# Six of the 2-MB weight loads of a mixture-of-experts kernel go out in three parts

## The chip, the cores and the metric

The kernel runs on one core of a Trainium2 chip. The metric is the device time of one execution in microseconds (us); lower is better. Three timed runs of the kernel before took 1313.0 to 1313.3 us, with a median of 1313.22 us. KB and MB in the rows are those of the profile: a load of "2048.0 KB" is 2,097,152 bytes.

## What is computed

One layer of a decoder over 512 tokens of width 1024: an attention part with two branches, then a mixture of 64 experts of which each token uses two, then a last norm. Cut to what the change is about:

```
def expert_block(args):            # D = 1024, D_EXPERT = 512
    xb, e = args
    return (jax.nn.silu(xb @ w1[e]) * (xb @ w3[e])) @ w2[e]

def reference(x, ...):
    h = rms_norm(x, attn_norm);  x = x + hybrid_mixer(h, ...)   # w_in, w_proj_fox, w_proj_swa, w_out
    h = rms_norm(x, ffn_norm);   x = x + hier_moe(h, ...)       # group top-1, expert top-2, expert_block
    return rms_norm(x, final_norm)
```

w1 and w3 are (64, 1024, 512), w2 is (64, 512, 1024), all float32: 2 MB for each matrix of each expert, 192 such matrices, 403 MB in all. Every one of them is read once.

## The kernel before

The first third of the span is the attention part. The experts follow in 16 batches of four (b = 0 to 15). Each expert has 32 token slots, so four experts fill the 128 partitions. A batch takes twelve 2-MB matrices: w1 of four experts (e = 0 to 3), w3 of four, w2 of four. TensorE multiplies them in float32 (`h` at L1571 from w1 and w3, `y_ps` at L1608 from w2), with the weights as the moving operand, and adds the batch's results to the token rows (`c_ps`, L1368).

The weights come from HBM by DMAs that SyncE (SP) issues in program order. `load_next` (L1028) issues one matrix as one DMA at L1038: 128 partitions, each a contiguous piece of 16 KB in HBM (for w1, partition p holds rows 8p to 8p+7). So a load is 128 packets of 16 KB. The tile comes from one of three rings (2, 4 and 2 tiles, `RING`), eight 2-MB tiles in all; a DMA into a tile waits until TensorE has read what was there before. `load_ahead` at the start of a batch issues as many loads as the rings allow. Batch 0 and the last batch's w2 are loaded in smaller parts by other functions. The landing of DMAs is told by eight semaphores in turn (DMAHW0 to DMAHW7 in the listings below): each DMA takes the next one and first waits for the DMA that had it before, eight DMAs earlier.

Other transfers that the prediction reads from: `raw_pf` (512 KB, 128 partitions) and `raw_ps` (twice 256 KB, 64 partitions each), both loaded at L174 in pieces of 1 KB as parts of the projection weights, and `fkl<-c_k` (L739), which moves four partitions of 2 KB within the core.

Of the kernel before, what the change touches and what calls it, by code (L numbers as in the profile page):

```python
# [20 lines left out]
P = 128  # L21
# [23 lines left out]
ANGLES_AT = 6  # L45
FORGET_AT = 13
ROUNDS = (5, 3)

CUTS = ((0, 512), (512, 768), (768, 1024))
BIG = 3e38  # L50
# [46 lines left out]
def kernel(ctx: ExitStack, tc: tile.TileContext, a: dict, out: bass.AP, dbg=None):  # L97
    nc = tc.nc
# [849 lines left out]
    w1, w3, w2 = a["w1"][0], a["w3"][0], a["w2"][0]  # L948
# [16 lines left out]
    def weights(m, x, k):  # L965

        w, n = {"w1": (w1, NC), "w3": (w3, NC), "w2": (w2, 4)}[m]
        rows = w[x].rearrange("(p c) n -> p c n", c=n)
        return rows if k is None else rows[:, k * n // 2:(k + 1) * n // 2]

    def note(b, m, k, e, rows):

        if k is None:
            wt[b, m, e] = rows
        else:
            wt.setdefault((b, m, e), [None] * (2 * len(rows)))[k * len(rows):(k + 1) * len(rows)] = rows

    def load_half(t, b, m, k, e):

        if (b, m, k) == (N_BATCH - 1, "w2", 1):  # L980

            src = w2[4 * b:4 * b + 4].rearrange("x (p c) n -> p c x n", c=4)
            if e < 2:
                t = t.rearrange("p (x n) -> p x n", x=4)
                nc.sync.dma_start(t, src[:, 2 + e, :, slice(*CUTS[0])])
                last[0, 2 + e] = [t[:, x] for x in range(4)]
                return
            t = t.rearrange("p (u x n) -> p u x n", u=2, x=4)
            for u in range(2):
                nc.sync.dma_start(t[:, u], src[:, 2 + u, :, slice(*CUTS[e - 1])])  # L990
                last[e - 1, 2 + u] = [t[:, u, x] for x in range(4)]
            return
        t = t.rearrange("p (c n) -> p c n", c=2 if m == "w2" else 4)
        nc.sync.dma_start(t, weights(m, 4 * b + e, k))
        note(b, m, k, e, [t[:, c] for c in range(t.shape[1])])
# [34 lines left out]
    def load_next():  # L1030

        i = len(issued) - n_first
        issued.append(i)
        t = rings[next_places[i % n_ring]].tile([P, 4096], F32, tag="ring", name=f"load{i}")
        if len(loads[i]) == 1 and loads[i][0][2] is None:
            b, m, k, e = loads[i][0]
            t = t.rearrange("p (c n) -> p c n", c=4 if m == "w2" else NC)
            nc.sync.dma_start(t, weights(m, 4 * b + e, k))  # L1038
            note(b, m, k, e, [t[:, c] for c in range(t.shape[1])])
            return  # L1040
        for u, x in enumerate(loads[i]):
            load_half(t[:, 2048 * u:2048 * u + 2048], *x)
# [23 lines left out]
    for n in range(4):  # L1066
# [5 lines left out]
        for m, src_hi, src_lo in (("pf", lambda k: ofT[k][0], lambda k: ofT[k][1]),  # L1072
                                  ("ps", lambda k: osT_hi[:, k], lambda k: osT_lo[:, k])):
            hi, lo = halves_of[f"{m}{n}"]
            for j in range(2):
                b = 2 * n + j
# [31 lines left out]
    def x1_part(n, t, o):  # L1108

        x1 = x1s[t % 2]  # L1110
        v.tensor_tensor(x1, o, xb_of[n][:, t], op=OP.add)
        act.activation(junk, x1, AF.Square, accum_out=sq4[:, t, n:n + 1])
# [64 lines left out]
    def route_places(t):  # L1177
        for x in range(2):
            v.scalar_tensor_tensor(junk[:, 0:N_EXP], pos_ps[t], 1.0, oh[:, x, t], op0=OP.mult, op1=OP.mult,
                                   accum_out=slots[:, x, t:t + 1])  # L1180
            yield
        yield from pick(t, slots, codes)
# [97 lines left out]
    def weave(rounds=1000):  # L1280

        for _ in range(rounds):
            for g in list(live):
                if next(g, "end") == "end":
                    live.remove(g)

    def later(n, g):
        for _ in range(n):
            yield
        yield from g  # L1290

    for t in range(NT):
        o = acc_tile(f"out_ps3_{t}")[:, :256]
        for cc in range(NC):
# [8 lines left out]
            if cc == 3 and t:  # L1303
                part_logits(3, t - 1)
                live.append(route_experts(t - 1))
                if t > 1:
                    route_count(t - 2)
                    live.append(later(1, route_places(t - 2)))
                weave(ROUNDS[t == 3])
        x1_part(3, t, o)  # L1310
# [242 lines left out]
    def load_ahead(n):  # L1553
        while len(issued) - n_first < min(n, len(loads)):
            load_next()
# [101 lines left out]
```

## Time and profile before

| what | us |
|---|---|
| median of three runs | 1313.22 |
| the profiled execution, its own time | 1313.3 |
| its span, first to last instruction | 1311.3 |
| around the span | 2.0 |

| engine | busy us | share of the span |
|---|---|---|
| TensorE matmuls | 1126.6 | 86% |
| VectorE | 457.5 | 35% |
| ScalarE | 245.7 | 19% |
| GpSimd | 73.6 | 6% |

The page also has a line for the core's 16 DMA engines: the span in 40 slices, with a digit for the busy share in tenths, and under it the GB/s that were moved. A busy share near 1.00 means that all 16 engines were moving a packet nearly all of the time.

### The profile page before, as it was taken

How to read it: one execution, taken by the hardware profiler on the slowest of the kernel's cores; microseconds unless marked ns; L12 is line 12 of the kernel's file. 1: busy time of each engine (PE TensorE's matmuls, PEld its weight loads, DVE VectorE, ACT ScalarE, POOL GpSimd, SP SyncE). 2: the span in 40 equal slices, each digit the busy share in tenths (PEclk: the TensorE clock that was granted, in tenths of full speed). 3: DMA queues.
4: the chain of work that ended last, by engine and by line, in shares of the span. 5: the costliest groups of instructions: out<-in, count | busy, mean ns of one | idle time of the engine just before them, and what ended most of it. 6: DMA issues, size and time to landing. Idle time of an engine off the chain costs nothing.

```text
span 1311.3 us, 16877 instructions
## 1 busy us (share of the span) xinstructions
PE 1126.6 (86%) x6934; PEld 610.5 (47%) x6934; DVE 457.5 (35%) x1138; ACT 245.7 (19%) x559; POOL 73.6 (6%) x100
## 2 busy tenths in 40 slices
PE   8999999999999797978879696968878786967865
PEld 8987777878984262413233241413232331413212
DVE  7776666236263362212303121212313121211113
ACT  5665444433541000000000000000000000000003
POOL 2700000012000000000000000000000000000002
PEclk9999999999999899979989898989889998989878
DMA  5222231356989999999999999999999999999995
GB/s 185 76 66 74 78 88 55 96 146 202 347 280 417 427 427 426 428 427 428 427 426 428 427 427 426 428 426 428 428 426 427 421 428 424 428 426 427 428 421 190
DMA packets 70074, 438.92 MB, mean 335 GB/s; under 512 B 9878, under 2 KB 39594, under 8 KB 45036
## 3 DMA queue, kind: packets, MB, share of 16 engines
q1 hardware_dynamic: 69994, 437.82, 82.3%
q8 instruction: 56, 0.92, 0.3%
q14 instruction: 22, 0.18, 0.0%
q10 hardware_dynamic: 2, 0.00, 0.0%
HBM read 433.48 MB, written 2.10 MB: 332 GB/s over the span
## 4 chain that ended last, share of the span: by engine, by line
PE 63%; DMA 31%; DVE 3%; SPq 1%; issue 1%; ACT 1%; POOL 1%; DVEq 0%; POOLq 0%; ACTq 0%
DMA load<-in_w_dram 30%; PE h L1571 11%; PE y_ps L1608 9%; PE g_ps L1261 9%; PE c_ps L1368 8%; PE acc_g L322 2%; PE acc_g L323 2%; PE acc_g L324 2%; SPq L1038 1%; PE of_ps L823 1%; PE acc_wo L324 1%; PE acc_kv L433 1%; PE acc_wo L322 1%; PE acc_wo L323 1%; PE fpT_ps L805 1%
## 5 line engine op out<-in xcount | busy, mean ns | idle before, releaser
L1571 PE MATMUL h<-load,u_hi 128*32 128x512 f32 x1920 | 293.3, 671 | 88.3 <-DMA load<-in_w_dram 88.1
L1608 PE MATMUL y_ps<-load,u_hi 128*32 128x512 f32 x920 | 167.9, 680 | 53.6 <-DMA load<-in_w_dram 50.3
L1571 PEld LDWEIGHTS h<-load,u_hi 128*32 128x32 f32 x1920 | 69.6, 121 | 288.4 <-issue 155.9
L1261 PEld LDWEIGHTS g_ps<-u_hi,xc 128*128 128x128 f32 x1024 | 118.8, 194 | 24.6 <-issue 13.0
L1261 PE MATMUL g_ps<-u_hi,xc 128*128 128x128 f32 x1024 | 124.9, 281 | 0.6 <-DVE over L1492 0.6
L1374 DVE TENSOR_TENSOR u_lo<-c_ps,u_lo 128x512 f32<-128x512 f32 x84 | 58.1, 692 | 188.3 <-PE c_ps L1368 188.3
L1608 PEld LDWEIGHTS y_ps<-load,u_hi 128*32 128x32 f32 x920 | 40.5, 117 | 168.8 <-issue 89.3
L1267 DVE TENSOR_TENSOR u_hi<-g_ps,cst 128x512 f32<-128x512 f32 (+1 forms) x33 | 21.9, 667 | 278.1 <-PE h L1571 261.5
L1368 PE MATMUL c_ps<-xb,xb 128*128 128x512 f32 x240 | 116.7, 617 | 1.0 <-DVE u_lo L1371 0.8
L1355 ACT ACTIVATE xb<-h 128x512 f32<-128x512 f32 x16 | 9.6, 597 | 355.9 <-PE h L1571 355.9
L1368 PEld LDWEIGHTS c_ps<-xb,xb 128*128 128x128 f32 x240 | 37.8, 188 | 79.4 <-DVE u_lo L1374 36.8
L1343 POOL TENSOR_TENSOR xb<-xb,u_hi 128x512 f32<-128x512 f32 x16 | 20.4, 1273 | 824.8 <-DVE xb L1342 748.4
L1365 ACT ACTIVATE xb<-y_ps 128x512 f32<-128x512 f32 x30 | 17.9, 597 | 216.4 <-PE y_ps L1608 216.4
L1362 ACT ACTIVATE u_hi<-t_ps 128x512 f32<-128x512 f32 x16 | 9.6, 597 | 255.3 <-PE t_ps L1361 255.3
L322 PE MATMUL acc_g<-hT_hi,hi_g 128*128 128x512 f32 x128 | 54.2, 423 | 0.0
L1211 DVE TENSOR_SCALAR u_hi<-codes,locs,cst 128x128 f32<-128x128 f32 x60 | 21.8, 363 | 87.5 <-PE g_ps L1261 87.5
L323 PE MATMUL acc_g<-hT_lo,hi_g 128*128 128x512 f32 x128 | 50.5, 395 | 0.0
L324 PE MATMUL acc_g<-hT_hi,lo_g 128*128 128x512 f32 x128 | 50.4, 394 | 0.0
L1356 DVE TENSOR_TENSOR u_hi<-h,xb 128x512 f32<-128x512 f32 x16 | 16.5, 1033 | 90.0 <-PE h L1571 89.1
L189 DVE TENSOR_TENSOR lo_g<-raw_g,hi_g 128x1024 fp32r<-128x1024 f32 x16 | 19.6, 1226 | 36.1 <-ACT hi_g L187 36.1
L322 PE MATMUL acc_wo<-hi_wo,mT 128*128 128x256 f32 x96 | 28.7, 299 | 0.0
L324 PE MATMUL acc_wo<-hi_wo,mT 128*128 128x256 f32 x96 | 27.1, 283 | 0.1
(377 smaller groups left out, 1604.3 us busy)
## 6 DMA issues: line engine op xcount, KB each, us to landing
load<-in_w_dram SPq DMA_DIRECT2D x176, 2048.0 KB
first<-in_w_dram SPq DMA_DIRECT2D x16, 1024.0 KB
load<-in_w_dram SPq DMA_DIRECT2D x9, 1024.0 KB
raw_g<-in_w_in_dram SPq DMA_DIRECT2D x16, 512.0 KB
raw_wo<-in_w_out_dram SPq DMA_DIRECT2D x8, 512.0 KB
x_sb<-in_x_dram SPq DMA_DIRECT2D x4, 512.0 KB
raw_qs<-in_w_in_dram SPq DMA_DIRECT2D x4, 512.0 KB
raw_vf<-in_w_in_dram SPq DMA_DIRECT2D x4, 512.0 KB
```

The source lines that it names most:

```text
L189: defer(wait, lambda: v.tensor_tensor(lo, r, hi.bitcast(F32), op=OP.subtract))
L322: pe.matmul(o, l_hi, r_hi, start=first, stop=False, skip_group_check=True)
L323: pe.matmul(o, l_hi, r_lo, start=False, stop=False, skip_group_check=True)
L324: pe.matmul(o, l_lo, r_hi, start=False, stop=last, skip_group_check=True)
L1211: v.tensor_scalar(sel1[:, t], labels, loc[:, 0, t:t + 1], r, op0=OP.is_equal, op1=OP.mult)
L1261: pe.matmul(g_ps[k][:, c * P:(c + 1) * P], xc[t][:, 4 * k + c], sel1[:, t], start=(t, c) == (0, 0), stop=t == NT - 1, skip_group_check=True)
L1267: v.tensor_tensor(hsel[:, d], g_ps[k][:, c * P:(c + step) * P].rearrange("p (c n) -> p c n", c=step), g_ffn[:, d, None].to_broadcast([P, s ...
L1343: gp.tensor_tensor(wsel, wsel, wtmp, op=OP.add)
L1368: pe.matmul(c_ps, w_t[:, t], ys[k], start=True, stop=True)
L1374: v.tensor_tensor(d, c_ps, d, op=OP.add)
L1571: pe.matmul(o[s], hsel[:, c, s], wt[b, m, e][c], start=c == 0, stop=c == NC - 1, skip_group_check=True)
L1608: pe.matmul(y_ps[k][s], gT[:, c, s], wt[b, "w2", e][c][:, 512 * k:512 * k + 512], start=c == 0, stop=c == 3, skip_group_check=True)
```

## The change

A list names six of the loads: the w1 matrix of the third expert (e = 2) in batches 1, 4, 6, 9, 11 and 14. Each of these goes out as three DMAs in place of one: partitions 0 to 111, then 112 to 119, then 120 to 127. The same bytes go to the same places; all other loads stay whole.

```
+UNEVEN = [(b, "w1", 2) for b in (1, 4, 6, 9, 11, 14)]
...
             t = t.rearrange("p (c n) -> p c n", c=4 if m == "w2" else NC)
-            nc.sync.dma_start(t, weights(m, 4 * b + e, k))
+            src = weights(m, 4 * b + e, k)
+
+            for p0, p1 in ((0, 112), (112, 120), (120, 128)) if (b, m, e) in UNEVEN else ((0, P),):
+                nc.sync.dma_start(t[p0:p1], src[p0:p1])
             note(b, m, k, e, [t[:, c] for c in range(t.shape[1])])
```

What SyncE issues around the first of the six (load4 is w1 of e = 2 in batch 1; a row is a DMA, its shape, and the semaphores that it waits for), before:

```order
L1038 DMA load3_4228<-in_w1_dram 128x4096 [waits DMAHW2_49,PE_49]
L1038 DMA load4_4230<-in_w1_dram 128x4096 [waits DMAHW3_49,PE_49]
L1038 DMA load5_4232<-in_w1_dram 128x4096 [waits DMAHW4_49,PE_49]
L1038 DMA load6_4392<-in_w3_dram 128x4096 [waits DMAHW5_49,PE_49]
L1038 DMA load7_4394<-in_w3_dram 128x4096 [waits DMAHW6_49]
```

And now, in the same place:

```order
L1043 DMA load3_4228<-in_w1_dram 128x4096 [waits DMAHW2_49,PE_49]
L1043 DMA load4_4230<-in_w1_dram 112x4096 [waits DMAHW3_49,PE_49]
L1043 DMA load4_4230<-in_w1_dram 8x4096 [waits DMAHW4_49]
L1043 DMA load4_4230<-in_w1_dram 8x4096 [waits DMAHW5_49]
L1043 DMA load5_4234<-in_w1_dram 128x4096 [waits DMAHW6_49,PE_49]
L1043 DMA load6_4394<-in_w3_dram 128x4096 [waits DMAHW7_49,PE_49]
L1043 DMA load7_4396<-in_w3_dram 128x4096 [waits DMAHW0_49]
```

One row has become three, and the loads behind it take semaphores two further on. On TensorE, the first products of batch 1 that use these loads, before:

```order
L1571 MATMUL h1_1_4468<-load2_4226,u_hi1_3867 32x512 [waits DMAHW1_49]
L1571 MATMUL h1_1_4468<-load3_4228,u_hi1_3867 32x512 [waits DMAHW2_49]
L1571 MATMUL h1_1_4468<-load4_4230,u_hi1_3867 32x512 [waits DMAHW3_49]
L1571 MATMUL h1_1_4468<-load5_4232,u_hi1_3867 32x512 [waits DMAHW4_49]
L1571 MATMUL h1_1_4468<-load2_4226,u_hi1_3867 32x512
```

And now:

```order
L1576 MATMUL h1_1_4470<-load2_4226,u_hi1_3867 32x512 [waits DMAHW1_49]
L1576 MATMUL h1_1_4470<-load3_4228,u_hi1_3867 32x512 [waits DMAHW2_49]
L1576 MATMUL h1_1_4470<-load4_4230,u_hi1_3867 32x512 [waits DMAHW5_49,DMAHW4_49,DMAHW3_49]
L1576 MATMUL h1_1_4470<-load5_4234,u_hi1_3867 32x512 [waits DMAHW6_49]
L1576 MATMUL h1_1_4470<-load2_4226,u_hi1_3867 32x512
```

The products stand in the same order; the first one on the split load waits for all three of its parts.

## Rows read from the trace of the kernel before

**Rows 1.** The page: span, and the chain that ended last, by engine and by line.

```profile
span 1311.3 us, 16877 instructions
...
PE 63%; DMA 31%; DVE 3%; SPq 1%; issue 1%; ACT 1%; POOL 1%; DVEq 0%; POOLq 0%; ACTq 0%
DMA load<-in_w_dram 30%; PE h L1571 11%; PE y_ps L1608 9%; PE g_ps L1261 9%; PE c_ps L1368 8%; PE acc_g L322 2%; PE acc_g L323 2%; PE acc_g L324 2%; SPq L1038 1%; PE of_ps L823 1%; PE acc_wo L324 1%; PE acc_kv L433 1%; PE acc_wo L322 1%; PE acc_wo L323 1%; PE fpT_ps L805 1%
```

**Rows 2.** Windows of the expert stage: busy us (instructions) by engine, clock, DMA share, GB/s.

```profile
core 0: us, PE busy (x) PEld busy (x) DVE busy (x) ACT busy (x) POOL busy (x), PEclk, DMA share, GB/s
440.00:500.00 60.00, 50.99 (x348) 26.80 (x348) 30.21 (x85) 2.99 (x5) 2.59 (x2) 0.91 1.01 427
...
800.00:900.00 100.00, 82.96 (x467) 30.82 (x460) 25.86 (x62) 5.16 (x9) 2.54 (x2) 0.93 1.01 427
...
1200.00:1260.00 60.00, 45.73 (x244) 12.12 (x240) 8.89 (x15) 2.88 (x5) 1.27 (x1) 0.86 1.01 427
```

**Rows 3.** Waits of TensorE and of SyncE's queue: us in total, times, longest.

```profile
PEld h L1571 <- DMA load<-in_w_dram: 119.4, 33, 4.9
PE h L1571 <- DMA load<-in_w_dram: 88.1, 29, 4.0
...
PEld y_ps L1608 <- DMA load<-in_w_dram: 73.0, 25, 3.9
```
```profile
SPq L1038 <- PE h L1571: 497.4, 37, 22.4
SPq L1038 <- PE y_ps L1608: 258.9, 29, 21.0
```

**Rows 4.** The chain in order of time, its end: start us, us, what.

```profile
1242.46 29.92 DMA load<-in_w_dram
1272.38 0.04 issue
1272.42 9.54 PE h L1571 x58
...
1284.47 5.41 PE y_psl L1417 x64
```

**Rows 5.** DMA issues of the whole loads: count and size; instruction ns min/median/max.

```profile
load<-in_w_dram SPq DMA_DIRECT2D x176, 2048.0 KB
```
```profile
L1038 SPq DMA_DIRECT2D load<-in_w_dram x176: 327/382/1492, 397.6 to 1242.5; - x176
```

**Rows 6.** DMA packets from 440 to 1260 us: by size; by queue (packets, MB, share).

```profile
DMA packets 24027, 349.88 MB, mean 427 GB/s; under 512 B 2669, under 2 KB 2669, under 8 KB 2670
...
q8 instruction: 31, 0.51, 0.3%
```

**Rows 7.** Windows within `raw_pf` (128 partitions), then within `raw_ps` (64 partitions).

```profile
256.75:257.50 0.75, 0.75 (x5) 0.57 (x5) 0.24 (x1) 0.48 (x1) 0.00 (x0) 1.00 1.08 380
267.75:268.50 0.75, 0.75 (x5) 0.61 (x4) 0.07 (x1) 0.65 (x1) 0.00 (x0) 1.00 1.05 373
...
261.00:262.00 1.00, 1.00 (x6) 0.81 (x5) 0.00 (x0) 0.69 (x1) 0.00 (x0) 1.00 0.97 236
272.00:273.25 1.25, 1.25 (x7) 1.03 (x6) 0.00 (x0) 0.69 (x1) 0.00 (x0) 1.00 1.05 240
```

**Rows 8.** DMA packets from 126 to 131 us, and all that was issued there.

```profile
DMA packets 544, 0.54 MB, mean 108 GB/s; under 512 B 24, under 2 KB 536, under 8 KB 544
...
raw_kf<-in_w_in_dram SPq DMA_DIRECT2D x1, 512.0 KB
fkl<-c_k SPq DMA_DIRECT2D x2, 8.0 KB
```

**Rows 9.** The last loads: DMA busy tenths in 40 slices from 1280 to 1295 us.

```profile
DMA  9999999999999998799999965555422100000000
```

## Prediction

> **What bounds the kernel now.** I read the page's chain first: of the 1311.3 us, 31% hang on DMA, nearly all of it on the expert weights [rows 1]. The windows then say where: from 440 to 1260 us the 16 DMA engines are busy with a share of 1.01 and move 427 GB/s in every stretch [rows 2]. That is a stage at its limit, not a stage that waits now and then. TensorE waits for loads all through it (119.4 + 73.0 us at the weight loads alone), while SyncE, which issues the loads, waits for TensorE to free tiles for 497.4 + 258.9 us [rows 3]. SyncE's long wait is no fault: the load issued at 1242.46 us ends a wait only at 1272.38 [rows 4], 29.92 us or about six loads later, so the queue always holds work for the engines. From this follow two rules for the sums. One: a load takes 2,097,152 B / 427 GB/s = 4.91 us, and each engine moves 8 of its 128 packets of 16 KB, 0.614 us each. Two: no engine has idle time in this stage, so whatever makes one engine later by 1 us in any load stays with it to the end, and a load counts as landed only when the last engine has its part. The end is set by the engine that is last after all loads; behind its landing at 1272.38 stands a tail of TensorE work that the change leaves as it is [rows 4].
>
> So the question is what the change does to the latest engine. Two readings bear on that. The packets under 512 B number 2669 in a stretch of 349.88 MB, which is 166.8 loads: 16.0 for each load, one landing note from each engine [rows 6]. And in the stretch with one 512-KB load and two transfers of four partitions there are 24 of them: 16, and 4 for each small transfer [rows 8]. A transfer of four partitions uses four engines. I take it that one of eight partitions uses eight, with one 16-KB row each, and that one of 112 uses all 16, with seven rows each (the trace has neither shape).
>
> **What the change adds and takes away.** Per split load, eight engines carry 7 + 1 + 1 = 9 rows in place of 8, the other eight carry 7. In the best case, every row still at 0.614 us, that is +0.61 us for one half and -0.61 us for the other; over six loads +3.7 and -3.7.
>
> [...]
>
> Whether the rows still run at 0.614 us is the costly term. The nearest rows are the transfers that reach only part of the partitions. While `raw_pf` comes in on 128 partitions, the engines are busy (1.08, 1.05) and move 380 and 373 GB/s; while `raw_ps`, the same packets on 64 partitions, comes in, they are as busy (0.97, 1.05) and move 236 and 240 [rows 7]. Busy engines at 63% of the rate are engines that hold each other up on the way into the 64 partitions: 3.7 GB/s for each partition reached, where the whole loads get 427/128 = 3.3. An 8-partition part moves 131,072 B. If the eight engines don't hold each other up, it takes 0.61 us; if the rate stays in proportion to the partitions, 8 x 3.7 = 29.8 GB/s and 4.4 us. Eight neighbouring partitions are the narrow case, so I take the middle, 2.5 us. Two parts: 5.0 us, with the seven rows before them 4.3 + 5.0 = 9.3 us against 4.91, so +4.4 us per load for the eight engines, +26.3 us over six.
>
> [...]
>
> Part of the 26.3 us may be covered. At the end of the last loads the busy share stands at 5 tenths from 1289.0 to 1290.5 us, after seven to nine tenths until 1288.6, and is gone after 1292.0 [rows 9] (0.375 us a slice): one half of the engines is done some 3.2 us before the last. If the eight engines with the extra rows are that early half, 3.2 us are free; if they are the late half, nothing. No row tells which, so I take 1.6 us: 24.7.
>
> The 112-row part has its own term. Its seven rows for each engine need not fall on the partitions that the engine fills in a whole load, so engines can meet there too. From below that is nothing (the 128-partition rate); from above, the 64-partition case at full loss, the seven rows take twice as long, +4.3 us per load. 112 partitions are near the 128 case, so I take a quarter, 1.07 us, 6.4 us over six. Engines that are still in the whole load ahead, or already in the next, would be met as well; I count this within the same bounds.
>
> Below nothing the two terms can't go: the bytes are the same and the engines already have a share of 1.01.
>
> The rest costs nothing, and I name its cover. Twelve more DMA issues at 0.38 us [rows 5] are 4.6 us of SyncE's time, under its 756 us of waiting. They stand ahead of the loads behind them by 0.76 us, under a lead of 29.92 us. A split load takes three of the eight landing semaphores, so the DMA eight behind waits for a load six back, not eight; with at most seven loads under way, that delays an issue by at most the 4.9 us of one load, again under the lead. If the lead were gone, each would cost its full length. TensorE waits for three semaphores at one product per split load; the gap after such a wait is 0.04 us [rows 4], six times nothing.
>
> The sum: 1313.3 us (the profiled execution's own time; the median is 1313.22) + 24.7 + 6.4 = **1344.4 us**.
>
> **The rivals.**
>
> *Balance (not slower).* The eight engines don't hold each other up: 16-KB rows come from HBM at 0.614 us each and find their way. Then the split only moves work from one half of the engines to the other, and if the extra rows go to the early half, the late half ends 3.7 us sooner and the early half 3.7 us later. For it speaks that there is a lasting cause for an early and a late half: 31 packets of 16 KB bring instructions, 0.3% of the engines' time, or about 39 us in 820 [rows 6]; on one half alone that is 4.9 us a head. With a lead of 3.2 us as in rows 9 the new last engine is 0.5 us later than now (1313.8); with 4.9 it is 1.2 us earlier (1312.1); with 7.4 or more, 3.7 earlier (1309.6). Against it speak rows 7. It decides at the price of a part: the extra per load is twice that price less 0.614 us, so from 0.79 us a part the kernel is slower by over 2.6 us even with the 3.2 us of cover.
>
> *The wrong half.* No holding up, but the extra rows go to the late half: the last engine is 3.7 us later, 1317.0 us.
>
> *It doesn't do what it says.* The 8-row parts are cut finer and go over all 16 engines; then every engine carries the same bytes as before and the time stays, 1313.3 us. Against it: the four-partition transfers with four notes each [rows 8].
>
> **How the numbers follow.** Holding up, 0.64: its own range goes from 1323 (parts at 1.4 us, nothing on the 112 rows, cover 3.2) to 1370 (parts at 4 us, 112 rows with 2 us a load: 6 x (4.3 + 2 + 8 - 4.91) = 56.3). Balance 0.20, of which 0.10 lies below 1310.7; the wrong half 0.08; no effect 0.08. About 0.2%, 2.6 us, is what a measurement of this kernel can tell from no change, so faster means below 1310.6: 0.10. Same, up to 1315.8: 0.10 + 0.08 = 0.18. Slower: 0.64 + 0.08 = 0.72. For 8 in 10 the range runs from 1311 (leaving out the 0.10 of faster) to 1370 (leaving out some 0.06 of the dearest).
>
> **What would show it.** If I am right, the windows that hold a split load (they land around 417, 593, 711, 887, 1005 and 1181 us in the trace of before) show a DMA share that stays near 1 while GB/s fall below 427, down to some 300 over two loads, and TensorE's waits for loads grow by about 31 us in all, in six places; the tail behind the last landing keeps its length, and the plateau at 5 tenths at the end moves or grows, since one half is now further apart from the other. In the balance case the GB/s stay at 427 everywhere and the plateau at the end shrinks or turns round. The forecast is wrong if 8-row parts land at the pace of whole loads; it is too low if the half that carries the seven rows is slowed as much as the other.

## The result and the profile after

| | before | after |
|---|---|---|
| median us | 1313.0 (1312.3 to 1313.3, 5 runs) | 1374.0 (1371.3 to 1377.5, 5 runs) |
| profiled execution, its span | 1313.3, 1311.3 | 1377.45 (the longest of the five), 1375.6 |

The kernel is slower: the ratio is 1.047 [1.0457, 1.0484], 61 us. The forecast was slower by 31, and its range ended at 1370. The sign and the place were right, the size was half.

In code the lines have moved by five: L1038 of before is L1043, L1571 is L1576, L1608 is L1613. The page of after, span and chain by engine; the row answers to [rows 1]:

```profile
span 1375.6 us, 16895 instructions
...
DMA 47%; PE 46%; DVE 2%; SPq 2%; issue 1%; ACT 1%; POOL 1%; DVEq 0%; POOLq 0%; ACTq 0%
```

DMA takes 47% of the chain, 31% before. Five of the ten windows of the expert stage, columns as in [rows 2]: us, busy us (instructions) of PE, PEld, DVE, ACT, POOL, granted clock, DMA share, GB/s:

```profile
440.00:500.00 60.00, 47.76 (x292) 25.05 (x292) 28.36 (x81) 2.39 (x4) 2.55 (x2) 0.83 1.01 427
500.00:600.00 100.00, 78.74 (x479) 26.88 (x478) 22.08 (x57) 5.76 (x10) 2.54 (x2) 0.91 1.01 418
...
700.00:800.00 100.00, 78.22 (x425) 26.47 (x423) 24.56 (x59) 6.36 (x11) 2.55 (x2) 0.89 1.01 388
...
900.00:1000.00 100.00, 78.77 (x393) 28.11 (x392) 21.38 (x51) 4.07 (x7) 1.27 (x1) 0.85 1.01 383
...
1200.00:1300.00 100.00, 71.04 (x386) 23.80 (x390) 15.20 (x34) 3.96 (x7) 2.54 (x2) 0.85 1.00 383
```

The last two columns are the point. The share stays at 0.98 to 1.01 in all ten windows, so the DMA engines are hardly ever idle, but where a split load lies they move less: 383 to 388 GB/s over 100 us, and 427 where none lies. Here the busy share does not tell a working engine from one that is held up; the GB/s do. Closer, around the first and the sixth split:

```profile
400.00:411.50 11.50, 9.56 (x88) 5.76 (x84) 3.27 (x10) 1.79 (x3) 1.26 (x1) 1.00 1.03 433
411.50:428.60 17.10, 16.34 (x105) 7.30 (x98) 6.57 (x8) 1.19 (x2) 0.00 (x0) 1.00 1.01 236
428.60:440.00 11.40, 9.97 (x70) 2.54 (x70) 2.74 (x3) 0.60 (x1) 0.00 (x0) 1.00 1.01 425
596.00:613.60 17.60, 17.58 (x90) 9.58 (x82) 6.57 (x11) 1.19 (x2) 0.00 (x0) 1.00 1.00 236
1222.80:1245.60 22.80, 22.21 (x108) 9.16 (x109) 5.53 (x8) 1.19 (x2) 0.00 (x0) 0.93 1.02 268
```

For 17.1 us all 16 engines together run at 236 GB/s, the rate that [rows 7] show for 64 partitions. The forecast had some 300 over two loads. The landing notes of single engines (16 for each whole load and for the 112-row part, eight for an 8-row part) show the same stretch load by load; times in us:

```
DMA                first engine   last engine
whole load ahead       411.40        416.90
112 partitions         419.08        426.89
8 partitions           420.87        425.50
8 partitions           423.39        426.73
whole load behind      428.58        431.56
```

From 411.40 to 428.58 is 17.2 us for two loads, 9.8 at the pace of before, and that is by the engine that lands first. The last engine of the whole load ahead is late already: 5.5 us behind the first, after 2.9 in the load before it. So all engines are held up, the ones with seven rows too, and whole loads beside the parts with them.

TensorE's waits for loads, in total, times, longest; the rows answer to [rows 3]:

```profile
PEld h L1576 <- DMA load<-in_w_dram: 168.1, 46, 4.8
PE h L1576 <- DMA load<-in_w_dram: 129.3, 44, 3.9
PEld y_ps L1613 <- DMA load<-in_w_dram: 74.6, 25, 4.3
```

The first went from 119.4 to 168.1 us and the second from 88.1 to 129.3; the third hardly moved. The end of the chain, as in [rows 4]:

```profile
1305.18 31.11 DMA load<-in_w_dram
1336.29 0.04 issue
1336.33 9.18 PE h L1576 x58
```

The last landing that ends a wait moved from 1272.38 to 1336.29, by 63.9 us, and the tail behind it is as long as it was (39.3 us to the end of the span, 38.9 before). All the loss lies in the stage.

The busy share behind the last loads, 1335 to 1350 us in 40 slices, as in [rows 9]:

```profile
DMA  9998999999999999999998433211105579950559
```

The plateau at 5 tenths is gone: the share falls to 4 tenths and on to nothing within 3 us. By the landings of the last whole load, the engines of before fall into a front half, within 2.8 us, and a back half, 4.1 to 6.4 us behind the first; those of after are fifteen within 1.9 us and a single one 9.9 us behind the first.

SyncE has a new wait, for landings of its own queue, which is not in [rows 3]:

```profile
SPq L1043 <- DMA load<-in_w_dram: 98.7, 15, 9.0
```

It is the wait that the forecast put at 4.9 us at most and under the lead; one is 9.0 us at most. The lead was not some 30 us everywhere. By the landings three whole loads of the change (landing around 885, 1016 and 1144 us) were issued 0.8 to 2.4 us after the first engine had finished the load ahead, and there the engines in front lost 2.3 to 4.0 us. The last engine, 8 us behind them, lost nothing (4.9 us from load to load there too), so these gaps cost nothing at the end.

### The profile page after: what moved, and what is told of

Its sections match the earlier page's. It is cut to its first block, busy times and chain, and to the rows that moved or that the text cites. A ratio compares the mean times of both kernels' runs of the same rounds, so it can differ in the third digit from the quotient of the medians.

```text
span 1375.6 us, 16895 instructions
## 1 busy us (share of the span) xinstructions
PE 1149.0 (84%) x6934; PEld 612.6 (45%) x6934; DVE 457.3 (33%) x1138; ACT 246.0 (18%) x559; POOL 73.5 (5%) x100
## 4 chain that ended last, share of the span: by engine, by line
DMA 47%; PE 46%; DVE 2%; SPq 2%; issue 1%; ACT 1%; POOL 1%; DVEq 0%; POOLq 0%; ACTq 0%
DMA load<-in_w_dram 46%; PE h L1576 10%; PE y_ps L1613 6%; PE g_ps L1266 3%; PE acc_g L324 2%; PE acc_g L325 2%; PE acc_g L326 2%; PE c_ps L1373 2%; SPq L1043 1%; PE of_ps L825 1%; PE acc_wo L326 1%; PE acc_kv L435 1%; PE acc_wo L324 1%; PE acc_wo L325 1%; PE fpT_ps L807 1%
## 5 line engine op out<-in xcount | busy, mean ns | idle before, releaser
L1576 PE MATMUL h<-load,u_hi 128*32 128x512 f32 x1920 | 317.0, 698 | 129.5 <-DMA load<-in_w_dram 129.3
L1576 PEld LDWEIGHTS h<-load,u_hi 128*32 128x32 f32 x1920 | 71.8, 125 | 355.3 <-issue 175.2
L1613 PE MATMUL y_ps<-load,u_hi 128*32 128x512 f32 x920 | 166.2, 669 | 54.5 <-DMA load<-in_w_dram 51.3
L1613 PEld LDWEIGHTS y_ps<-load,u_hi 128*32 128x32 f32 x920 | 40.0, 116 | 168.6 <-issue 87.5
L325 PE MATMUL acc_g<-hT_lo,hi_g 128*128 128x512 f32 x128 | 50.5, 395 | 0.0
```

The lines of the kernel that those rows point to most:

```text
L325: pe.matmul(o, l_hi, r_lo, start=False, stop=False, skip_group_check=True)
L1576: pe.matmul(o[s], hsel[:, c, s], wt[b, m, e][c], start=c == 0, stop=c == NC - 1, skip_group_check=True)
L1613: pe.matmul(y_ps[k][s], gT[:, c, s], wt[b, "w2", e][c][:, 512 * k:512 * k + 512], start=c == 0, stop=c == 3, skip_group_check=True)
```

## The experiments

The theory was that parts which reach few partitions make engines hold each other up ("crowding", later "meeting"); the rivals were that each extra DMA costs something by itself ("pieces"), that it is a matter of how many engines carry a part ("count"), and that the 112-row part is to blame ("shift"). All edits are to the list of parts in `load_next`; the six loads are those of the change unless another list is given. Times stand against the runs of before on the same chip (1311.9 to 1312.6).

### Do three DMAs cost anything by themselves?

Run e1_cols3 cuts the same loads in three along the columns:

```diff
-            for p0, p1 in ((0, 112), (112, 120), (120, 128)) if ... else ((0, P),):
-                nc.sync.dma_start(t[p0:p1], src[p0:p1])
+            for c0, c1 in ((0, 4), (4, 6), (6, 8)) if ... else ((0, t.shape[1]),):
+                nc.sync.dma_start(t[:, c0:c1], src[:, c0:c1])
```

> The six loads again go out as three DMAs, but cut along the columns: each part reaches all 128 partitions, with 8 KB, 4 KB and 4 KB of every row. Crowding (my theory: parts that reach few neighbouring partitions make the engines hold each other up): about the time of before, 1313 us, at most 1318. Pieces (rival: what costs is two more DMAs per load, with their issues, landing notes and waits, whatever they reach): like the change, about 1374 us, which is 5.1 us for each of the twelve extra DMAs.

Measured: 1314.2 us, ratio 1.0013 [1.0003, 1.0023], 1.9 us for twelve extra DMAs with their issues, notes and waits. "Pieces" falls. It is the cut into blocks of partitions that costs.

### Which part costs it?

```diff
-((0, 112), (112, 120), (120, 128))
+((0, 112), (112, 128))
```

> The 112 partitions stay one DMA, the last 16 partitions go out as one DMA in place of two. Crowding at the small parts: 16 neighbouring partitions at 3.7 GB/s each take 4.4 us, half of two such parts, so about half of the 61 us stays: 1335 to 1350. Pieces: half as well, 1343. Shift (rival: it is the 112-row part, whose seven rows for each engine fall out of step with the eight of a whole load): nearly all of it stays, 1365 to 1375. If the small parts cost only because eight engines carry them while eight stand by: about 1313 to 1318, since 16 rows give each engine one.

Measured: 1364.9, ratio 1.0399 [1.0382, 1.0416]. Of 61 us 52.6 are left with one 16-row part. A DMA of 16 rows leaves 16 landing notes (`stage<-in_b_gate`, L211 of before), so I take it that each engine has a row of this part. My expectation of about half missed: that there are two narrow parts is not the main thing. The time lies at the edge of what "shift" named (1365 to 1375).

Two runs with five parts follow, of the same sizes, once on neighbouring partitions and once spread:

```diff
# e3_near5
+((0, 64), (64, 96), (96, 112), (112, 120), (120, 128))
# e4_far5: every 2nd, 4th, 8th, 16th, 16th partition
+for h, r in ((0, 2), (1, 4), (3, 8), (7, 16), (15, 16)) if ... else ((0, 1),):
+    ti, si = [x.rearrange("(i r) c n -> i r c n", r=r)[:, h] for x in (t, src)]
+    nc.sync.dma_start(ti, si)
```

> The six loads go out in five parts of 64, 32, 16, 8 and 8 neighbouring partitions. Crowding: each part reaches only its share of the partitions, at most 4.4 us each, 22 us in all in place of 4.9 if nothing overlaps; as the parts overlap I expect 6 to 15 us per load, 1350 to 1405. Pieces: four extra DMAs at 5.1 us, six times: 1435. Shift: no 112-row part is left; parts of 64, 32 and 16 are out of step too, 1374 or more.

> The same five parts by size (64, 32, 16, 8, 8 rows), but each spread over all 128 partitions: every 2nd, 4th, 8th, 16th and 16th. Every DMA has as many rows as in the run with neighbouring partitions, so as many engines. Crowding: the loss is gone, 1313 to 1325 (the two 8-row parts still move 3.7 us from one half of the engines to the other). Pieces or engine count: the same time as with neighbouring partitions. Shift: about 1313 too, since the rows of each engine lie where a whole load has them.

Measured: 1389.0, ratio 1.0566 [1.0533, 1.0599], with neighbours; 1337.6, ratio 1.0190 [1.0173, 1.0207], spread. Rows and number of DMAs are the same, and so, by an estimate from the landing notes (16 for 64 rows and for 16 rows in the trace of before, eight for eight rows in that of the change), are the engines; so 51 us hang on which partitions a part takes, and "count" falls. But the spread parts were not free either: 25 us, above the 13 that I had allowed. The landings of the first split, on the middle engine, show where: the 64-row part follows the load ahead by 2.45 us and the 32-row part by another 1.7 (2.46 and 1.23 at 0.614 us a row), while the 16-row part takes 1.2 and the 8-row parts 0.6 and 1.1 in place of 0.6 each. Spacing isn't enough; it has to be the right one.

### What does each shape cost?

Run e5_shapes leaves the computation out and measures shapes one after another, in fourteen stages. Its core, cut:

```
for name, parts in STAGES:
    for r in range(3):
        for _ in range(3):
            load((whole,))
        load(parts)
    for _ in range(3):
        t = load((whole,))
    nc.sync.dma_start(out2[rows:rows + 16], t[0:16, 0:1024])   # waits for the last load
```

> A kernel of loads alone: nothing is computed, the output is not the reference's. Fifteen stages; in each, three times three whole 2-MB loads and then one load in the stage's parts, then three more whole loads and a wait until all have landed. The extra of a stage is its length over the stage of whole loads, a third of it per load in parts; 'alone' leaves the other rows out. Meeting (theory: a whole load gives each engine a place of its own in the partitions, and parts that don't make engines meet): 112 alone takes 7 to 10 us in place of 4.3, so it is dear by itself; the two 8-row parts on neighbouring partitions alone take 3 to 9 us, the same two with every 4th partition 1.2 us on eight engines, with every 16th some 2.4; two halves of 64 neighbours cost 4.9 us extra, even and odd partitions about nothing. Count (rival: what decides is how many engines a part uses and how many parts there are): 112 alone takes 4.3 us, the 8-row parts cost the same with any spacing, both ways of 64 and 64 cost nothing.

Windows within eight of its stages: us, busy of POOL, clock, DMA share, GB/s. In this order: whole loads; 112, 8, 8; 112 alone; the two 8-row parts alone; two 8-row parts with every 4th partition alone; 112, 16; two halves of 64; even and odd partitions.

```profile
10.00:77.10 67.10, 0.00 (x0) 1.00 1.01 430
82.00:174.80 92.80, 0.00 (x0) 1.00 1.01 324
180.00:262.80 82.80, 0.00 (x0) 1.00 1.01 347
268.00:335.80 67.80, 0.00 (x0) 1.00 0.99 361
341.00:397.90 56.90, 0.00 (x0) 1.00 0.99 424
472.00:560.80 88.80, 0.00 (x0) 1.00 1.01 329
635.00:729.70 94.70, 0.00 (x0) 1.00 1.01 309
735.00:803.30 68.30, 0.00 (x0) 1.00 1.01 428
```

The share says 0.99 to 1.01 in all of them; 309 to 430 GB/s say how different they are. The length of a stage, from the last landing of the stage before to its own, gives the time of one load in parts: a stage of even and odd halves is 73.6 us, which is 15 loads at 4.90, so a third of what another stage takes beyond that, added to 4.9, is its load (the first stage, of whole loads, is no base, since the start is in it):

| parts | stage us | time of the load in parts | its rows at 0.614 us, on the engine with most (estimate) |
|---|---|---|---|
| 112, 8, 8 | 97.8 | 13.0 | 5.5 |
| 8, 8, 112 | 96.3 | 12.5 | 5.5 |
| 112 alone | 88.0 | 9.7 | 4.3 |
| 8, 8 neighbours alone | 72.5 | 4.5 | 1.2 |
| 8, 8 every 16th alone | 68.6 | 3.2 | 1.2 |
| 8, 8 every 4th alone | 62.5 | 1.2 | 1.2 |
| 112, 16 | 94.4 | 11.8 | 4.9 |
| 16 neighbours alone | 69.0 | 3.4 | 0.6 |
| 64, 64 halves | 99.8 | 13.6 | 4.9 |
| 64 even, 64 odd | 73.6 | 4.9 | 4.9 |
| 96 alone | 95.4 | 12.2 | 3.7 |
| 96, 32 | 102.4 | 14.5 | 4.9 |
| 120, 8 | 111.9 | 17.7 | 5.5 |

Three readings. The 112-row part alone takes 9.7 us: 5.4 over its rows, more than the 4.3 that the forecast took as its worst. Eight-row parts on neighbours take 4.5 for the two, near the forecast's 5.0; with every 4th partition they cost no more than their rows, and in the landings eight engines fall back by 0.61 us a part and the other eight by nothing. And 64 even with 64 odd rows is free where two halves of 64 take 13.6 us, so neither the row count nor the small size decides.

That engines meet when each has seven rows is my reading of this. The whole loads at 427 GB/s agree with engines that don't meet. If seven rows go to each engine in order, the bounds between engines fall elsewhere than with eight; but no row here shows which engine wrote which partition, in a whole load or in a part, and that engines meet there is argued and not shown.

Two halves in the full kernel, beside even and odd, decide it there:

```diff
# e8_even_odd
+for h, r in ((0, 2), (1, 2)) if ... else ((0, 1),):       # loop body as in e4_far5
# e15_halves
+((0, 64), (64, 128))
```

> The six loads go out as two DMAs, one on the even partitions and one on the odd ones. With loads alone this cost nothing. Meeting: 1312 to 1315. If parts cost something in the full kernel that they don't cost with loads alone (TensorE's waits, the landing notes): 5 us a split as for the other parts, 1340.

> The six loads go out as two halves of 64 neighbouring partitions. Meeting: with loads alone this cost 8.7 us a load (a stage 26 us longer than with even and odd partitions), so 52 us or more, 1365 to 1395, while even and odd cost nothing with the same number of DMAs, rows and engines. Small parts (rival: only parts of few rows are dear): 1312 to 1320.

Measured: even and odd 1312.7, ratio 1.0002 [0.9993, 1.0011]; halves 1362.3, ratio 1.0374 [1.0358, 1.0390], 49.7 us or 8.3 a load. The number of DMAs and the rows of each are the same, and so is the number of engines: the packets under 512 B, 2753 in 349.96 MB and 2577 in 328.34, are 16 notes for each load and 16 more for each that goes out in two. DMA over 440 to 1260 us, GB/s in 40 slices, even and odd first, then halves:

```profile
GB/s 428 424 428 425 429 426 428 426 428 426 428 427 426 428 427 428 425 430 425 429 423 432 424 430 424 429 425 429 425 430 426 427 427 428 415 428 428 425 430 423
```
```profile
GB/s 425 429 426 428 426 428 427 335 359 428 426 429 421 352 320 427 427 428 425 427 428 425 377 276 429 421 425 373 430 263 405 407 409 416 385 428 425 428 302 371
```

Even and odd show nothing at all. With halves the five deep dips (335, 320, 276, 263, 302) stand where the second to sixth split stand, and behind the dip at the fifth split (263) the rate stays at 385 to 416 for some 100 us. There the engines in front fall back by 6 us towards the last one, which loses nothing. (The profiled execution of the halves is the longest of its five, 1374.4 us.) What "meeting" said of the shapes holds, in the kernel as with loads alone: the choice of partitions decides.

One rival no run keeps apart. With the partitions the pieces of HBM change too: a half reads 1 MB in one piece, the even partitions every second 16 KB of 2 MB. Two readings of the kernel before speak against HBM as the place. `raw_pf` and `raw_ps` read the same pattern, 1 KB out of every 4 KB, and only the one on 64 partitions falls to 236 GB/s [rows 7]. And while `x_sb` comes in, a block of 128 token rows, 512 KB that are one piece of HBM, on all 128 partitions, the engines move 373:

```profile
10.20:11.20 1.00, 0.86 (x6) 0.65 (x6) 1.00 (x2) 1.00 (x2) 1.00 (x1) 1.00 0.97 373
```

### Eight-row parts with the free spacing, in the kernel

```diff
+steps = [slice(0, P, 2), slice(1, P, 4)] + [slice(a, a + 29, 4) for a in (3, 35, 67, 99)]
+for s in steps if ... else (slice(0, P),):
+    nc.sync.dma_start(t[s], src[s])
```

> The six loads go out as six DMAs: the 64 even partitions, 32 partitions (every 4th from 1), and four 8-row parts with every 4th partition (from 3, 35, 67 and 99). Each 8-row part again uses eight engines, so these carry 4+2+4 = 10 rows and the others 6; with 0.61 us a row that moves 1.2 us a load, 7.4 us over six, from one half of the engines to the other. Meeting gone, eight engines the early half: 7.4 us less the 2 to 4 us by which they are ahead, 1315 to 1319. The same on the late half: 1319 to 1321. If 8-row parts hold the engines up in the full kernel whatever their spacing, as the forecast had it (2.5 us a part, four parts): 10 - 4.9 x 10/8 + 3.7 = 7.5 us a load, about 1357.

Measured: 1335.8, ratio 1.0175 [1.0161, 1.0189], 23 us: neither of my cases. DMA from 400 to 440 us, one slice a us:

```profile
GB/s 418 467 483 393 442 442 393 475 442 377 426 426 393 475 426 410 262 246 246 279 262 426 377 475 377 410 492 393 426 442 377 475 426 377 492 377 426 442 377 492
```

The 64-row and the 32-row part run at full rate; from 416 to 421 us it is 246 to 279. Seen by landings, on the middle engine, the four 8-row parts take 0.6, 0.9, 1.3 and 1.2 us. Only eight engines carry each of them (by the eight notes of an 8-row part), and the other eight are in the next whole load by then. That these meet in partitions 67 to 127 fits; it was argued from the landings, not tested.

### Does each split cost the same?

```diff
-UNEVEN = [(b, "w1", 2) for b in (1, 4, 6, 9, 11, 14)]
# e6_one
+UNEVEN = [(b, "w1", 2) for b in (1,)]
# e7_late_one
+UNEVEN = [(b, "w1", 2) for b in (14,)]
```

> Only the first of the six loads is split. If each split costs the same and nothing is covered: 61/6 = 10.2 us, 1323. If the first costs what its landings show in the trace of the change (two loads in 17.2 us instead of 9.8 on the fastest engine): 7.4 us, 1320. If the cost grows because engines that lie apart from an earlier split meet worse in the next: under 6 us, 1315 to 1319. If there is a cover of up to 3.2 us at the end as the forecast assumed, it shows here at once: 1316 to 1320.

> Only the last of the six loads is split. In the trace of the change the first split holds the last engine up by 7.4 us and the sixth by 13.4, while the engines already lie 5 us apart ahead of it. If the rise comes from the earlier splits (engines that an earlier split has pulled apart meet worse): 1318 to 1320, as with the first one alone (1318.5). If it comes from the place in the stage (the instruction fetches alone pull the engines apart by then): 1321 to 1326.

Measured: the first alone 1318.5, ratio 1.0050 [1.0036, 1.0063], 6.5 us; the last alone 1325.5, ratio 1.0095 [1.0080, 1.0111], 13.1. The first lies between two of my cases, 7.4 us as in its landings and under 6 us with a cost that grows from split to split, and decides for neither. The second falls in the case of the place in the stage: the rise does not need earlier splits. A difference between the two places is the distance between the first and the last engine two loads ahead: 1.3 us at the first, 5.6 at the last. In the trace of before it grows the same way, from 2.3 to 6.4 us, and with 30 of the 31 instruction packets [rows 6] the landings of a load come 1.4 to 1.7 us later, summed over its 16 engines: one engine at a time falls back.

Run e10_spread makes that distance with loads alone (again nothing is computed), with extra 8-row parts of the free spacing between the whole loads ahead:

```
LATE = tuple(slice(32 * (k // 4) + k % 4, 32 * (k // 4) + k % 4 + 29, 4) for k in range(4))
...
load((W,)); load(LATE[:late]); load((W,)); load(parts)      # for late = 8, LATE twice
```

> Loads alone again, nothing is computed. Each stage: three whole loads, the load in parts, four whole loads, a wait for all. Between the whole loads ahead stand 0, 2, 4 or 8 extra 8-row parts with every 4th partition, which make eight engines 0, 1.2, 2.5 or 4.9 us late and cost nothing else. The cost of a shape is its stage less the stage of a whole load in its place with the same lateness. Spread (theory: parts out of step cost more, the further apart the engines are, since late engines are still in the load ahead while early ones are in the parts): 112, 8, 8 costs 6 to 8 us with engines level and 11 to 13 with 4.9 us between them, 112 alone rises likewise, even and odd stays at nothing. Rival (the dearer splits late in the kernel have to do with its other traffic, as instruction fetches): the cost is the same for all four, within 1.5 us.

Measured as laid down there, a stage less the stage of a whole load with as many extra parts (for none, less eight loads at 4.9 us), for 0, 2, 4 and 8 extra parts; the two shapes "alone" leave the other rows out:

| parts | 0 | 2 | 4 | 8 |
|---|---|---|---|---|
| 112, 8, 8 | 8.1 | 9.7 | 10.3 | 10.0 |
| 112 alone | 3.6 | 5.1 | 7.0 | 8.3 |
| 8, 8 alone | -0.5 | -0.3 | -0.3 | -0.3 |
| even and odd | 0.1 | 0.8 | 0.0 | -0.4 |

The two shapes with 112 rows rise by 2.2 and 4.7 us, so the rival (the same within 1.5 us, and dear only beside other traffic) falls; the 8-row parts alone don't rise. But nothing comes to the 11 to 13 that I had expected. The extra parts did not make the distances that I had meant either: in the stages of even and odd partitions, which disturb nothing, the engines lay 1.9, 3.7, 5.2 and 4.6 us apart. And the late engines are here always the eight that carry 8-row parts, so the run shows the rise and not its size in the kernel.

The next two runs take the distance away in the kernel. Ahead of the late split a small copy is issued that reads an earlier load:

```diff
+            if (b, m, e) == (14, "w1", 0):
+                drained = moe.tile([P, 4], F32, name="drained")
+                nc.sync.dma_start(drained, newest[0][:, 0:4])     # newest: tile of the load before
```

> No load is split. Two loads ahead of the place of the sixth split SyncE waits once until all loads under way have landed (a small copy reads the newest of them), so that all engines start level again. This is the control for the next run: the drain costs the distance between the engines (up to 6 us) and the time until the next load moves, 5 to 12 us: 1318 to 1324.

> The same drain, and the sixth of the six loads is split, as in the run with the last one alone, which cost 13.1 us. Spread (the split is dearer late in the kernel because the instruction fetches have pulled the engines 5 us apart by then): with level engines the split costs what the first one cost, 6 to 7 us over the control. Place (something else late in the kernel makes it dearer): again about 13 us over the control.

In the program the copy comes behind one more load, so that load stayed under way: in the control the engines in front ran dry for 2.9 us and the last one lost nothing. The control, window by window around it:

```profile
1160.00:1170.00 10.00, 6.67 (x34) 1.83 (x22) 5.62 (x18) 1.08 (x2) 1.27 (x1) 1.00 1.01 431
1170.00:1180.00 10.00, 8.09 (x55) 2.55 (x56) 0.00 (x0) 1.19 (x2) 0.00 (x0) 1.00 0.92 374
1180.00:1190.00 10.00, 9.98 (x40) 4.46 (x39) 5.53 (x8) 0.00 (x0) 0.00 (x0) 1.00 1.00 426
```

Measured: control 1312.9, ratio 1.0002 [0.9993, 1.0011]; with the split 1319.4, ratio 1.0053 [1.0039, 1.0067]. The split costs 6.5 us over the control, as the first one did, where it cost 13.1 without the drain. (Its profiled execution is the longest of its five, 1323.2.) The control is worth a look: 10 us at a DMA share of 0.92 cost nothing; by the landings the last engine never stood still. From 1177 to 1206 us, the late split first without the drain, then with it:

```profile
1177.00:1206.00 29.00, 23.51 (x122) 11.53 (x121) 5.53 (x8) 1.19 (x2) 0.00 (x0) 0.90 1.01 254
```
```profile
1177.00:1206.00 29.00, 23.96 (x126) 11.66 (x125) 5.53 (x8) 1.19 (x2) 0.00 (x0) 0.94 1.01 303
```

Last, the same with all six splits; five drains, since the first split finds level engines anyway. The edit is the list of places:

```diff
-            if (b, m, e) == (14, "w1", 0):
+            if (b, m, e) in [(x, "w1", 0) for x in (4, 6, 9, 11, 14)]:
```

> Control: no load is split; ahead of the places of the second to sixth split SyncE waits once for the load two ahead of the one that went out last, so that the engines that are in front run dry for some 3 us and the late ones hardly. One such drain cost 0.7 us: five cost 0 to 6 us, 1312 to 1319.

> All six loads are split as in the change, with the drains of the control ahead of the second to sixth. Spread: every split costs about what the first one costs, 6 x 6.5 = 39 us over the control, about 1353. Place, or earlier splits: 55 to 61 over the control, 1368 to 1375.

Measured: control 1312.6, ratio 1.0000 [0.9991, 1.0009]; with the splits 1363.1, ratio 1.0372 [1.0358, 1.0387], 50.5 us over the control, between the two theories. The drains take 11 of the 61 us away. By the landings, on the last engine over the load ahead, the split one and the load behind, beyond three loads at 4.9 us:

| split | 1 | 2 | 3 | 4 | 5 | 6 | sum |
|---|---|---|---|---|---|---|---|
| the change | 7.4 | 8.4 | 10.9 | 12.8 | 10.4 | 12.9 | 62.8 |
| with drains | 7.7 | 8.2 | 10.6 | 9.2 | 8.3 | 8.5 | 52.5 |

The last three splits, ahead of which the engines of the change lay 4 to 6 us apart, get cheaper by 2.1 to 4.4 us each, the first three don't. So the distance between engines is shown as a cause of the rise, and for 11 us of it. The change has drains of its own, too: where the load around 1016 us came late, the distance fell from 8.2 to 4.0 us, and the fifth split behind it is cheaper than the fourth and the sixth. In the control the five drains bring the engines only from 2.8 to 3.9 us apart to 2.3 to 3.0 (the front ones give up 0.6 to 1.5 us each time, the last at most 0.7), where the single drain brought them from 5.1 to 2.2; whether that is why the third to sixth split still cost 8.3 to 10.6 by the landings stays open.

No version came out that beats the kernel before: the cheapest forms, even and odd halves and the drain, equal it.

## Why the prediction was too low, step by step

- **The stage and its rules.** Right. Lateness is carried to the end one to one: in the profiled executions the last engine is 62.8 us later by the six splits, 63.9 at the last landing that ends a wait, and the span is 64.3 longer, with the tail unchanged. That no engine has idle time holds for the last engine only: around 1036 us of before a load was issued just 0.6 us before the first engine was through with the one ahead, and its landings are 8.8 us later, summed over the engines.
- **Eight rows use eight engines.** Right: each such DMA leaves eight landing notes with data, and with every 4th partition eight engines fall back by 0.61 us a part, the others by nothing; so there both parts fall on the same eight, as the sum had taken it.
- **The 8-row parts, 2.5 us each.** About right, a little high: 4.5 us for two alone, and 3.3 of the 13.0 us when they follow the 112 rows (13.0 less 9.7).
- **The 112-row part.** This is the term that failed. It was taken at a quarter of the loss of 64 partitions, 1.07 us a load, with 4.3 as the end, because "112 partitions are near the 128 case". Alone it loses 5.4 us (in the stages with extra parts 4.2 to 8.9, more with the distance between engines), and 112 with 16 rows in the kernel loses 52.6 us over six, 8.8 a load. What counts is not how many partitions a DMA reaches, as 64 even and 64 odd rows show; that seven rows for each engine make engines meet is the reading that fits, argued as said above and not shown. With 5.4 in its place and 3.3 for the two parts the sum per load is 9.7 + 3.3 - 4.9 = 8.1, six times 48.6 us, and the forecast would have been 1362. The 12 us that are left are of the size of what the distance between engines costs, 11 us by the drains; that they are the same is not shown.
- **Neighbours "within the same bounds".** Failed. The whole load ahead was slowed by the part behind it, and this grows with the distance between engines: 6.5 us for the first split, 13.1 for the same split late in the stage. The forecast knew of the early and the late half [rows 9], but used it only as a cover.
- **The cover of 1.6 us.** Failed in kind. There is slack: the front engines lost 2.9 us in the one drain, and 0.6 to 1.5 us in each of five, at no cost. But the split holds up all engines, the last one too, so its price doesn't go where the slack is. In the run with the first split alone the last engine lands 6.9 us later than before just behind the split, and 6.9 us later at the last whole load: none of it was covered.
- **Issues, semaphores, waits: nothing.** Right in the sum: 1.9 us for the column cut, 0.4 for even and odd. Its bounds were wrong: a wait for a landing was 9.0 us at most and not 4.9, and the lead ran out in three places, without a loss at the end.
- **The rivals.** Balance needed 8-row parts at the pace of whole loads. That pace exists with every 4th partition (1.2 us for two parts), but not for neighbours (4.5), and the 112-row part would have sunk it anyway. The other two did not occur.
- **What would show it.** The share near 1 with falling GB/s, the six places and the unchanged tail came as named; the waits of TensorE grew by 50 us in PEld's rows and not by 31. The plateau did not come as named: it neither grew nor moved but went, since after the splits one engine is late and not a half. The sentence that the forecast "is too low if the half that carries the seven rows is slowed as much as the other" is what happened.

## What to carry to other kernels

Where loads run at the limit of the DMA engines, cut them along the columns, or into even and odd partitions, and not into blocks of partitions: for six loads the first two cost 0 to 2 us here, the third 50 to 77 for the same bytes. Read GB/s beside the DMA share, since a share of 1 covered everything from 236 to 430 GB/s here. And price a shape that the trace doesn't hold with a kernel of loads alone before trusting an interpolation between the shapes it does hold.

## What the hardware showed that I had not expected

- A DMA of 112 partitions is no seven eighths of one with 128: 9.7 us against 4.9; 96 alone took 12.2, and 120 with 8 took 17.7, the dearest shape of all (120 rows leave fifteen landing notes with data, so they use fifteen engines).
- Two DMAs of 64 even and 64 odd partitions run at 428 GB/s, two of 64 neighbours count as 154 (2 MB in 13.6 us), with equal rows, packets and number of engines.
- Engines that are ahead can stand still without loss (a share of 0.92 over 10 us cost nothing), and with engines 5 us apart the same split cost twice as much (13.1 us) as with engines 1.3 us apart or after a drain (6.5).
- Instruction packets of 16 KB pull the engines apart: 31 of them in 820 us, each with some 1.5 us on one engine, and in the trace of before the first and the last end 6.4 us apart.
